# A two-layer hybrid decoder on one core: first products of a weight unit copied between PSUM banks, gates summed in PSUM, and another order of products

## The chip, the core and the metric

The kernel runs on one core of a Trainium2 chip, as one program for the whole computation. The metric is the device time of one execution in microseconds (us). The core has in-order engines that work side by side: TensorE (PE) multiplies matrices and adds the products up in PSUM banks, VectorE (DVE) does sums and differences, ScalarE (ACT) does copies, casts and the silu, GpSimd (POOL) and SyncE (SP) do the rest, SP mostly issuing DMAs of weights. An engine that has come to an instruction whose input isn't ready waits there, with all that is queued behind it.

## What is computed

Two decoder layers on 16 meta tokens and 512 tokens (528 in all, of width 1024), float32. The change touches the FFN alone:

```python
def hybrid_layer(h, ...):
    ...
    h = h + jnp.einsum('blc,cd->bld', mix, w_out)
    hn = rmsnorm(h, ffn_norm_g)
    ff = jax.nn.silu(jnp.einsum('bld,df->blf', hn, w_gate)) * jnp.einsum('bld,df->blf', hn, w_up)
    return h + jnp.einsum('blf,fd->bld', ff, w_down)
```

The width of `ff` is 2816. Ahead of it in a layer stand an RMSNorm, an input projection, attention with forgetting gates beside retention in chunks, and the output projection `w_out`. After the second layer come a last RMSNorm and the drop of the meta tokens. Layer 0 computes 528 tokens and layer 1's FFN the 512 that are returned.

## The kernel before

**Precision.** Each float32 matrix is split into a hi part (a cast on ScalarE: `whi`, `fwhi`, `th`, `ah`) and a lo part (the rest, a difference on VectorE: `wlo`, `fwlo`, `tl`, `al`), and each product is three matmuls: hi by hi, hi by lo, lo by hi. The weights' tiles lie in two rings, `whi`/`wlo` with two slots and `fwhi`/`fwlo` with three, between which the list of jobs alternates. When TensorE's program comes to a job's first matmul, `need` converts the jobs that come next in the list (L941 the cast, L942 the difference).

**Units.** The 2816 columns are 22 tiles f of 128, each with a gate and an up part. Tiles 0 and 1 are computed plainly (L231, finished at L895 and L896). Tiles 2 to 21 are *units*: gate and up together by seven products in place of eight, in a scheme of Strassen's kind over two halves of the width and two halves of the tokens (264 tokens each in layer 0, 256 in layer 1). A product (`product`, L953) is 12 matmuls, four steps of the width by three. Its weights are one of four forms: w1 the gate weights (`make1`), w2 (`make2`, L1084 and L1085), w3 (`make3`, L1092) and w4 (`make4`, L1098). Its right sides are halves of the normed input or forms of it (`x_forms`, L905 to L919, eight times ahead of the units: a scaled copy on ScalarE, four sums on VectorE, a split).

A unit has three PSUM banks: x, from the pool `psa` of four single banks, and z and y, the two of one tile of the pool `psd` of two tiles. The first product goes to x and is kept in memory by ScalarE (`keep`, L1117); x goes on to collect further products and is kept twice more; z and y collect one and two products. At the end `done` (L1127) takes z and y plus the kept copies as the gate (`sg`, L1131 and L1133), silu, multiplies it with the up part (L1136, L1138, L1139), and splits the result into `ah` and `al`.

**Fills.** The down projection of a group of tiles (`ROUNDS`) is spread between the products of the next group's units. In the groups f = 2 to 9 and 14 to 17 a unit carries two regular fills d0 and d1: `place` copies a slice of h into PSUM banks (p0 and p1, L1191 or L1193), the chunks of six matmuls add to it (L1207; two chunks for f = 2 to 5, four for the others), and ScalarE copies it back (L1214 or L1216). In the groups f = 10 to 13 and 18 to 21 the fill is a `Pair`, again seven products in place of eight, of six matmuls each (d0 to d6), whose results VectorE adds to h (L1036 to L1041). The down projection of the last group runs behind the units, in layer 0 with L1207 and in layer 1 as the tail, with `product` and the last norm woven in.

**Order.** TensorE's order is written out by hand in the loop at L1229 to L1265: x and z of the two first units ahead (x z x z), then for each unit (its own x and z first, from f = 4 on) x2 (w2), y (w2), p0, x3 (w3), d0, x (w3), p1, y (w4), d1. The orders of VectorE, ScalarE and SP are made by the framework's scheduler from the order of the calls, the estimated times and the marks `high_priority`.

Of the kernel before, what the change touches and what calls it, by code (L numbers as in the profile page):

```python
# [10 lines left out]
F32 = mybir.dt.float32  # L11
F32R = mybir.dt.float32r
AF = mybir.ActivationFunctionType
ALU = mybir.AluOpType
# [27 lines left out]
def hybrid_kernel(ctx, tc, x_t, w_in, w_fl, w_out, w_gate, w_up, w_down, vecs, b_fg, rope, decay, mask, ident, out_t):  # L42
# [818 lines left out]
    def ffn(l, st, real, last):  # L861
# [43 lines left out]
        def x_forms(k):  # L905
            def go():
                if k == 0:
                    st["t"] = [[fft(f"t{p}{i}", shape=(128, 2, 4, w)) for p in "hl"] for i in range(2)]
                s = fft("S", F32, (128, 6, w), 2)
                a, b = ((h[k][:, c0:c1], h[HB + k][:, c0:c1]) for c0, c1 in HC)  # L910
                g0, g1 = vcol(V_FFN + l * NK + k), vcol(V_FFN + l * NK + HB + k)
                with tc.issue_after(st["scaled"].ins) if real else ExitStack():
                    nc.scalar.activation(s[:, 0:2], two(h[k]), AF.Copy, scale=g0)
                nc.vector.tensor_sub(s[:, 2], s[:, 1], s[:, 0])
                for i in range(2):
                    nc.vector.scalar_tensor_tensor(s[:, 3 + i], b[1], g1, s[:, 1 + i], ALU.mult, ALU.subtract)
                nc.vector.scalar_tensor_tensor(s[:, 5], a[1], g1, s[:, 4], ALU.mult, ALU.subtract)
                th, tl = (t[:, k % 2] for t in st["t"][k // 2])
                split(th, tl, s[:, 2:6])  # L919
# [72 lines left out]
        class Pair:  # L992
# [40 lines left out]

            def add(self, i, col, n):
# [20 lines left out]
        class Unit:  # L1055
# [4 lines left out]

            def rest(self):
                self.w2 = add_job(load=self.load, make=self.make2, n=NK)
                self.w3 = add_job(load=self.load, make=self.make3, n=NK)
# [48 lines left out]
            def keep(self, i):  # L1112
                def go():
                    if i == 0:
                        self.t["e"] = fft("e", F32, (128, 3, w), 2)
                    with tc.high_priority():
                        nc.scalar.copy(self.t["e"][:, i], self.t["x"][:, 0:w])  # L1117
                        if i == 2:
                            e3 = self.t["e"][:, 2]
                            y = self.t["y"][:, 0:w]  # L1120
                            if self.f < PLAIN + 2:
                                y = tt("sq")[:, 0:w]
                                nc.scalar.copy(y, self.t["y"][:, 0:w])
                            nc.vector.tensor_add(e3, y, e3)
# [520 lines left out]
```

## Time and profile before

| what | us |
|---|---|
| runs | 1253.14, 1255.43, 1255.62 |
| median | 1255.43 |
| profiled execution | 1253.98 |
| its span | 1252.2 |
| TensorE busy in it | 1238.8 |
| VectorE busy | 1033.8 |
| ScalarE busy | 786.5 |

The span is that of the core's instructions; the execution's time has 1.8 us around it. A page of the profile has the busy time of each engine, then the granted clock of TensorE and the loads in 40 slices, the chain of work that ended last, and the costliest groups of instructions. A row such as `922.20 0.68 DVE L895 ... tq<-psd,R 128x512` says: from 922.20 us on, for 0.68 us, VectorE ran an instruction of line 895, that wrote the tile `tq` from a PSUM tile and `R`. A bracket behind it tells how long the engine sat idle before, and what released it. An instruction's duration includes its ends, which overlap the next one, so that starts stand closer than durations. An `x12` at the end of a row of TensorE joins 12 matmuls.

### The profile page before, as it was taken

The numbers are of one execution on the slowest core, as the hardware profiler recorded it, in microseconds if no ns is written. First come the engines' busy times: TensorE is split into PE (matmuls) and PEld (weight loads), VectorE is DVE, ScalarE is ACT, GpSimd is POOL, SyncE is SP. The second block draws the span as 40 slices with busy tenths as digits, with TensorE's granted clock in tenths as the row PEclk, the third lists the DMA queues.
The fourth block names the chain that finished last, engine by engine and source line by source line (L and its number), as shares of the span: only waits on it lengthen the run. The fifth ranks groups of instructions, "written<-read, shape, count | busy, mean of one in ns | idle before, by whom it ended". The sixth has DMA issues, their size and how long they took to land.

```text
span 1252.2 us, 24704 instructions
## 1 busy us (share of the span) xinstructions
PE 1238.8 (99%) x9609; PEld 1203.0 (96%) x9609; DVE 1033.8 (83%) x1969; ACT 786.5 (63%) x1525; POOL 293.6 (23%) x568
## 2 busy tenths in 40 slices
PE   9999999999999999999999999999999999999997
PEld 8999999999999999999999988998899999999997
DVE  7887756889987999799876877567999789988996
ACT  7766655677765645565566665557767665556545
POOL 4555655440000000000045556554300000000000
PEclk9999999999999999999999999999999999999999
DMA  6222222122433233322312222221414333332322
GB/s 237 68 71 75 77 69 85 60 85 70 143 110 102 85 102 119 102 85 85 118 61 85 75 79 69 77 84 52 142 57 140 102 102 102 102 110 93 102 68 68
DMA packets 43349, 116.27 MB, mean 93 GB/s; under 512 B 5088, under 2 KB 9952, under 8 KB 43232
## 3 DMA queue, kind: packets, MB, share of 16 engines
q1 hardware_dynamic: 42800, 114.41, 28.8%
q8 instruction: 75, 1.23, 0.4%
q14 instruction: 42, 0.34, 0.1%
q10 hardware_dynamic: 432, 0.29, 0.1%
HBM read 112.58 MB, written 2.10 MB: 92 GB/s over the span
## 4 chain that ended last, share of the span: by engine, by line
PE 92%; DVE 4%; ACT 2%; DMA 1%; issue 0%; SPq 0%; ACTq 0%; DVEq 0%
PE psd L231 28%; PE psa L953 23%; PE psd L953 16%; PE psd L1207 8%; PE psa L231 5%; PE psa L1207 3%; PE psa L452 2%; PE psa L619 2%; PE psa L549 1%; PE psa L753 1%; PE psa L789 1%; DMA raw<-w_down 1%; DMA h<-x_t 1%; PE psa L312 0%; DMA raw<-w_in 0%
## 5 line engine op out<-in xcount | busy, mean ns | idle before, releaser
L208 POOL TENSOR_TENSOR wlo<-raw,whi 128x128 fp32r<-128x128 f32 x488 | 253.7, 554 | 214.2 <-ACT whi L204 196.5
L231 PE MATMUL psd<-xh,whi 128*128 128x264 f32 (+1 forms) x696 | 169.5, 313 | 0.0
L231 PE MATMUL psd<-xl,whi 128*128 128x264 f32 (+1 forms) x696 | 160.6, 300 | 0.4 <-DVE xl L351 0.4
L231 PE MATMUL psd<-xh,wlo 128*128 128x264 f32 (+1 forms) x696 | 160.8, 300 | 0.0
L231 PEld LDWEIGHTS psd<-xh,whi 128*128 128x128 f32 x696 | 112.3, 189 | 3.3 <-ACT whi L204 0.3
L231 PEld LDWEIGHTS psd<-xh,wlo 128*128 128x128 f32 x696 | 110.9, 188 | 4.4
L231 PEld LDWEIGHTS psd<-xl,whi 128*128 128x128 f32 x696 | 111.5, 189 | 3.4 <-DVE xl L351 0.8
L204 ACT CAST whi<-raw 128x512 fp32r<-128x512 f32 (+1 forms) x140 | 82.2, 612 | 33.1 <-PE psd L231 17.4
L941 ACT CAST fwhi<-raw 128x512 fp32r<-128x512 f32 (+2 forms) x88 | 66.0, 757 | 51.7 <-PE psd L953 30.1
L942 DVE TENSOR_TENSOR fwlo<-raw,fwhi 128x512 fp32r<-128x512 f32 (+2 forms) x88 | 75.1, 854 | 20.9 <-ACT fwhi L941 20.6
L127 POOL MEMSET kc<- 64x528 f32 x4 | 2.1, 534 | 367.5 <-PE psd L1207 367.4
L941 ACT CAST whi<-raw 128x1024 fp32r<-128x1024 f32 (+1 forms) x72 | 56.1, 788 | 26.2 <-PE psd L953 17.6
L1117 ACT COPY e<-psa 128x264 f32<-128x264 f32 (+1 forms) x120 | 44.9, 374 | 42.6 <-PE psa L953 42.6
L953 PE MATMUL psa<-th,fwhi 128*128 128x264 f32 (+1 forms) x248 | 70.6, 285 | 0.0
L953 PE MATMUL psa<-th,fwlo 128*128 128x264 f32 (+1 forms) x248 | 70.2, 283 | 0.0
L953 PE MATMUL psa<-tl,fwhi 128*128 128x264 f32 (+1 forms) x248 | 70.2, 283 | 0.0
L953 PE MATMUL psa<-th,whi 128*128 128x264 f32 (+1 forms) x232 | 65.5, 282 | 0.0
L953 PE MATMUL psa<-th,wlo 128*128 128x264 f32 (+1 forms) x232 | 65.4, 282 | 0.0
L953 PE MATMUL psa<-tl,whi 128*128 128x264 f32 (+1 forms) x232 | 65.4, 282 | 0.0
L566 ACT ACTIVATE pr<-pr,nmax 128x144 f32<-128x144 f32 (+1 forms) x64 | 36.8, 576 | 45.4 <-DVE nmax L553 26.0
L942 DVE TENSOR_TENSOR wlo<-raw,whi 128x1024 fp32r<-128x1024 f32 (+1 forms) x72 | 64.0, 891 | 1.1 <-ACT whi L941 0.9
L953 PE MATMUL psd<-xh,fwlo 128*128 128x264 f32 (+1 forms) x168 | 47.6, 283 | 0.0
(445 smaller groups left out, 4417.7 us busy)
## 6 DMA issues: line engine op xcount, KB each, us to landing
raw<-w_in SPq DMA_DIRECT2D x54, 512.0 KB, 3.5
raw<-w_gate SPq DMA_DIRECT2D x44, 512.0 KB, 3.6
fraw<-w_up SPq DMA_DIRECT2D x40, 512.0 KB, 3.5
raw<-w_down SPq DMA_DIRECT2D x80, 256.0 KB, 3.6
raw<-w_out SPq DMA_DIRECT2D x16, 512.0 KB, 3.5
h<-x_t SPq DMA_DIRECT2D x8, 264.0 KB, 5.1
dec<-decay SPq DMA_DIRECT2D x8, 264.0 KB, 2.8
raw<-w_up SPq DMA_DIRECT2D x4, 512.0 KB, 3.9
```

Source lines behind the costliest of these rows:

```text
L204: pin(nc.scalar.copy(hi, job["raw"][:, c0:c1]), pinned)
L208: pin(sub(lo[:, c:c + step], job["raw"][:, c0 + c:c0 + c + step], hi[:, c:c + step].bitcast(F32)), pinned)
L231: nc.tensor.matmul(ps[1][b][:, 0:c1 - c0], w[:, wk, :], x[:, c0:c1], start=(k == 0 and i == 0), stop=(k == n - 1 and i == 2))
L452: nc.tensor.transpose(ps[:, 128 * j:128 * j + 128], src[:, o:o + 128], idt)
L549: nc.tensor.matmul(sc[0:nq, 0:c1 - c0], qq[:, q0:q0 + nq], kk[:, c0:c1], start=(i == 0), stop=(i == 1))
L566: nc.scalar.activation(pr, pr, AF.Exp, bias=nmax[0:nq], scale=-1.0, accum_out=rsum)
L619: nc.tensor.matmul(po[:, c0:SEQ], v[:, j, :], pp[:, j, META + c0:T], start=(j == 0 and i == 0), stop=(j == 4))
L941: nc.scalar.copy(hi, src)
L942: nc.vector.tensor_sub(lo, src, hi.bitcast(F32))
L953: nc.tensor.matmul(bank()[:, 0:b.shape[-1]], a[:, o + k, :], b, start=(fresh and k == 0 and i == 0), stop=(k == n - 1 and i == 2), skip_gr ...
L1117: nc.scalar.copy(self.t["e"][:, i], self.t["x"][:, 0:w])
L1207: nc.tensor.matmul(v[:, 0:c1 - c0], a[:, s * n + k, :], b[:, c0:c1], start=(k == 0 and i == 0 and not kept), stop=(k == n - 1 and i == 2), ...
```

## The change

- **Kept by a copy from bank to bank.** A unit's first product x is copied by ScalarE into the bank z, and the second product adds to it. The first product of y is copied to memory (`e`), and then VectorE writes x + e into the bank y, and later x + e into `e`, the second up part. So z and y collect the whole gate in PSUM, and `gated` reads it with the scaling in one instruction (L1143 of the changed kernel) as soon as its last product is in, ahead of the unit's last product. A `Pair`'s first product is likewise copied from x to z, where VectorE added it before.
- **Order of a unit.** xx, y, z, p0, x2, d0, p1, x3, d1, y2, x4 with regular fills, and xx, d0, y, x2, z, d2, d1, d3, x3, d4, y2, d5, x4, d6 with a `Pair` (before: x, z, d0, x2, y, d2, x3, d1, d3, x, d4, y, d5, d6). Here y is w2, z w1, x2 w2, x3 w3, y2 w4 and x4 w3. The first two units' heads are x, x, z, z. In the job list the fill stands behind w2 and before w3.
- **Temporaries.** The tile `S` of `x_forms` has four parts in place of six (the scaled copy goes to a tile `z`), and `e` one part in place of three. The last norm's temporaries, which shared these tiles, are allotted to fit (not shown).

The matmuls are the same in number and form.

```diff
@@ -906,17 +906,18 @@
 ...
-                s = fft("S", F32, (128, 6, w), 2)
+                s = fft("S", F32, (128, 4, w), 2)
+                sc = two(tt("z"))
-                    nc.scalar.activation(s[:, 0:2], two(h[k]), AF.Copy, scale=g0)
+                    nc.scalar.activation(sc, two(h[k]), AF.Copy, scale=g0)
 ...
@@ -1031,6 +1032,11 @@
                     return self.t[n]
                 return go
 
+            def keep(self):
+                z, x = (self.bank(n)()[:, 0:w] for n in "zx")
+                with tc.high_priority():
+                    nc.scalar.copy(z, x)
+
 ...
@@ -1044,9 +1050,9 @@
 ...
-                return (product(self.w1, 0, b(0, 0), x, True, False, 2, self.add(0, 0, "x")),
+                return (product(self.w1, 0, b(0, 0), x, True, False, 2, self.keep),
                         product(self.w1, 4, form(r, 2), x, False, False, 2, self.add(0, 1, "x")),
-                        product(self.w1, 2, b(1, 0), z, True, True, 2),
+                        product(self.w1, 2, b(1, 0), z, False, True, 2),
                         product(self.w1, 6, form(r, 1), y, True, False, 2, self.add(1, 1, "y")),
                         product(self.w2, 0, form(r, 3), x, False, False, 2, self.add(1, 1, "x")),
                         product(self.w2, 4, b(1, 1), y, False, True, 2, self.add(0, None, "zy")),
@@ -1111,32 +1123,34 @@
 
             def keep(self, i):
                 def go():
-                    if i == 0:
-                        self.t["e"] = fft("e", F32, (128, 3, w), 2)
+                    z, y, x = (self.bank(n)()[:, 0:w] for n in "zyx")
                     with tc.high_priority():
-                        nc.scalar.copy(self.t["e"][:, i], self.t["x"][:, 0:w])
-                        if i == 2:
-                            e3 = self.t["e"][:, 2]
-                            y = self.t["y"][:, 0:w]
-                            if self.f < PLAIN + 2:
-                                y = tt("sq")[:, 0:w]
-                                nc.scalar.copy(y, self.t["y"][:, 0:w])
-                            nc.vector.tensor_add(e3, y, e3)
+                        if i == 0:
+                            nc.scalar.copy(z, x)
+                        elif i == 1:
+                            self.t["e"] = fft("e", F32, (128, 272), 2)[:, 0:w]
+                            nc.scalar.copy(self.t["e"], y)
+                        elif i == 2:
+                            nc.vector.tensor_add(y, x, self.t["e"])
+                        else:
+                            nc.vector.tensor_add(self.t["e"], x, self.t["e"])
                 return go
 
+            def gated(self):
+                sg = self.t["sg"] = tt("sg")
+                c = slice(t0, T)
+                with tc.high_priority():
+                    nc.vector.scalar_tensor_tensor(two(sg), self.t["zy"][:, :, 0:w], RSC, two(st["R"]), ALU.mult, ALU.mult)
+                silu(sg[:, c], None if self.f < NF - 1 else ROOTS if last else LOGS)
+                u = self.t["u"] = tt("tq")
+                nc.vector.scalar_tensor_tensor(u[:, c], sg[:, c], RSC, st["R"][:, c], ALU.mult, ALU.mult)
+
             def done(self):
-                e = self.t["e"]
-                sg = tt("sg")
-                with tc.high_priority():
-                    nc.vector.tensor_add(two(sg), self.t["zy"][:, :, 0:w], e[:, 0:2])
+                u = self.t["u"]
                 c = slice(t0, T)
-                nc.vector.scalar_tensor_tensor(sg[:, c], sg[:, c], RSC, st["R"][:, c], ALU.mult, ALU.mult)
-                silu(sg[:, c], None if self.f < NF - 1 else ROOTS if last else LOGS)
-                u = tt("tq")
-                nc.vector.scalar_tensor_tensor(u[:, c], sg[:, c], RSC, st["R"][:, c], ALU.mult, ALU.mult)
                 u2 = two(u)
                 nc.vector.tensor_mul(u2[:, 0], self.t["x"][:, 0:w], u2[:, 0])
-                nc.vector.tensor_mul(u2[:, 1], e[:, 2], u2[:, 1])
+                nc.vector.tensor_mul(u2[:, 1], self.t["e"], u2[:, 1])
 ...
@@ -1149,20 +1163,17 @@
                 token_forms(self.f, u2)
 
             def head(self):
-                x, y, z = (self.bank(n) for n in "xyz")
-                return (product(self.w1, 0, x_block(0, 0), x, True, False, done=self.keep(0))
-                        + product(self.w1, HB, x_block(1, 0), z, True, True))
-
-            def middle(self):
+                x, z = (self.bank(n) for n in "xz")
+                return (product(self.w1, 0, x_block(0, 0), x, True, False, done=self.keep(0)),
+                        product(self.w1, HB, x_block(1, 0), z, False, True))
+
+            def rows(self):
                 x, y = (self.bank(n) for n in "xy")
-                return (product(self.w2, 0, t_form(2), x, False, False, done=self.keep(1))
-                        + product(self.w2, HB, t_form(0), y, True, False)
-                        + product(self.w3, 0, t_form(1), x, False, False, done=self.keep(2)))
-
-            def tail(self):
-                x, y = (self.bank(n) for n in "xy")
-                return (product(self.w3, HB, t_form(3), x, False, True)
-                        + product(self.w4, 0, x_block(1, 1), y, False, True, done=self.done))
+                return (product(self.w2, HB, t_form(0), y, True, False, done=self.keep(1)),
+                        product(self.w2, 0, t_form(2), x, False, False, done=self.keep(2)),
+                        product(self.w3, 0, t_form(1), x, False, False, done=self.keep(3)),
+                        product(self.w4, 0, x_block(1, 1), y, False, True, done=self.gated),
+                        product(self.w3, HB, t_form(3), x, False, True, done=self.done))
 
@@ -1237,11 +1247,12 @@
-                for i in (f, f + 1) if f == PLAIN else (f,):
-                    if i not in units:
-                        units[i] = Unit(i)
-                        steps += units[i].head()
-                u = units[f]
+                if f == PLAIN:
+                    units = {i: Unit(i) for i in (f, f + 1)}
+                    heads = [u.head() for u in units.values()]
+                    steps += heads[0][0] + heads[1][0] + heads[0][1] + heads[1][1]
+                u = units.get(f) or Unit(f)
+                xx, z = ([], []) if f < PLAIN + 2 else u.head()
                 p, g0, g1 = fills.pop(0)
                 seven = r - 1 in SEVENTHS and p in SEVEN
                 after = r - 1 in SEVENTHS and p + 1 in SEVEN or r in SEVENTHS and f == f1 - 1 and 0 in SEVEN
@@ -1251,17 +1262,18 @@
                     pair.rest()
                     u.last()
                     jobs[u.w3]["reach"] = 5 if after else 4
-                    d, m, t = pair.steps(), u.middle(), u.tail()
-                    steps += d[0] + m[:NK] + d[2] + m[NK:] + d[1] + d[3] + t[:HB] + d[4] + t[HB:] + d[5] + d[6]
+                    d, (y, x2, x3, y2, x4) = pair.steps(), u.rows()
+                    steps += xx + d[0] + y + x2 + z + d[2] + d[1] + d[3] + x3 + d[4] + y2 + d[5] + x4 + d[6]
-                u.rest()
+                u.second()
                 j = down_job(p, g0, g1)
                 jobs[j]["reach"] = 4 if after else 3
+                u.third()
                 u.last()
                 (p0, d0), (p1, d1) = (down(j, s, 2 * p + s, g0, g1, b, True)
                                       for s, b in enumerate((not real or f < PLAIN + 2, f == PLAIN)))
-                m, t = u.middle(), u.tail()
-                steps += m[:NK] + [p0] + m[NK:] + d0 + t[:HB] + [p1] + t[HB:] + d1
+                y, x2, x3, y2, x4 = u.rows()
+                steps += xx + y + z + [p0] + x2 + d0 + [p1] + x3 + d1 + y2 + x4
             fills = [(p, f0, f1) for p in range(NK // 2)]
```

**First place: the start of layer 1's FFN.** On ScalarE, before, from the cast of the input form of the last step but one to the hi part of the second weight form of f = 2 (`e` keeps x, `psa<-h0` is p0):

```order
L155 CAST th1_12030<-S_12105 128x1024
L1117 COPY e_12181<-psa_12168 128x256
L155 CAST th1_12030<-S_12132 128x1024
L1191 COPY psa_12261<-h0_73 128x256
L1191 COPY psa_12262<-h0_73 128x256
L941 CAST whi_12161<-S_12163 128x1024
```

and in the changed kernel (L1129 is the copy of x into z, of the first and the second unit):

```order
L1202 COPY psa_12232<-h0_73 128x256
L1129 COPY psd_12165<-psa_12152 128x256
L1202 COPY psa_12233<-h0_73 128x256
L1129 COPY psd_12187<-psa_12174 128x256
L155 CAST th1_12010<-S_12115 128x1024
L155 CAST ah1_12133<-tq_12130 128x512
L942 CAST whi_12145<-S_12147 128x1024
```

The two copies, of which the second waits for the second unit's x, now both stand ahead of the casts `th1`, `ah1` and `whi`. On VectorE, before, from the product of the plain tile 1 (L895) to the lo part of that weight form:

```order
L895 SCALAR_TENSOR_TENSOR tq_12146<-psd_12113,R_12018 128x512
L1084 TENSOR_TENSOR S_12163<-fraw_12070 128x512
L917 SCALAR_TENSOR_TENSOR S_12132<-h7_80,vec_84,S_12132 128x256
L1085 TENSOR_TENSOR S_12163<-S_12163,raw_12068 128x512
L1092 TENSOR_TENSOR fraw_12070<-raw_12068,fraw_12070 128x512
L155 TENSOR_TENSOR tl1_12031<-S_12132,th1_12030 128x1024
L896 TENSOR_TENSOR tq_12146<-tq_12146,sg_12102 128x512
L942 TENSOR_TENSOR wlo_12162<-S_12163,whi_12161 128x1024
```

and in the changed kernel:

```order
L895 SCALAR_TENSOR_TENSOR tq_12130<-psd_12096,R_11998 128x512
L917 SCALAR_TENSOR_TENSOR S_12115<-h7_80,vec_84,S_12115 128x256
L155 TENSOR_TENSOR tl1_12011<-S_12087,th1_12010 128x1024
L918 SCALAR_TENSOR_TENSOR S_12115<-h7_80,vec_84,S_12115 128x256
L1096 TENSOR_TENSOR S_12147<-fraw_12051 128x512
L896 TENSOR_TENSOR tq_12130<-tq_12130,sg_12084 128x512
L1097 TENSOR_TENSOR S_12147<-S_12147,raw_12049 128x512
L155 TENSOR_TENSOR tl1_12011<-S_12115,th1_12010 128x1024
L1104 TENSOR_TENSOR fraw_12051<-raw_12049,fraw_12051 128x512
L943 TENSOR_TENSOR wlo_12146<-S_12147,whi_12145 128x1024
```

The lo part `wlo` has two scaled steps (L917, L918) and a split of 1024 columns (`tl1_12011`) more behind L895 than before, and make3's step (L1104) still ahead of it.

**Second place: VectorE around the unit f = 4 of layer 1.** Before, from the lo part of w3 of f = 4, behind the gate of f = 3, to the sum x + y of f = 4 (L1124); `raw_12589` and `fraw_12591` are the weights of f = 5:

```order
L942 TENSOR_TENSOR wlo_12504<-fraw_12425,whi_12503 128x1024
L1085 TENSOR_TENSOR S_12626<-S_12626,raw_12589 128x512
L1136 SCALAR_TENSOR_TENSOR tq_12482<-sg_12478,R_12018 128x512
L942 TENSOR_TENSOR wlo_12571<-raw_12423,whi_12570 128x512
L1138 TENSOR_TENSOR tq_12482<-psa_12201,tq_12482 128x256
L1139 TENSOR_TENSOR tq_12482<-e_12214,tq_12482 128x256
L1092 TENSOR_TENSOR fraw_12591<-raw_12589,fraw_12591 128x512
L1098 TENSOR_TENSOR raw_12589<-raw_12589,S_12626 128x512
L155 TENSOR_TENSOR al3_12487<-tq_12482,ah3_12486 128x512
L942 TENSOR_TENSOR fwlo_12669<-fraw_12591,fwhi_12668 128x1024
L1124 TENSOR_TENSOR e_12521<-psd_12523,e_12521 128x256
```

and in the changed kernel, up to the sum that goes to the bank y of f = 4 (L1134). Directly ahead of these rows stand the lo part `fwlo_12504` of w3 of f = 4 (128x1024) and the gate of f = 3 (L1143, 128x512). `raw_12569` and `fraw_12571` are the weights of f = 5, `raw_12733` and `fraw_12735` those of f = 6:

```order
L943 TENSOR_TENSOR fwlo_12574<-raw_12569,fwhi_12573 128x1024
L1146 SCALAR_TENSOR_TENSOR tq_12461<-sg_12458,R_11998 128x512
L943 TENSOR_TENSOR wlo_12485<-raw_12481,whi_12484 128x512
L1152 TENSOR_TENSOR tq_12461<-psa_12174,tq_12461 128x256
L1153 TENSOR_TENSOR tq_12461<-e_12365,tq_12461 128x256
L1097 TENSOR_TENSOR S_12605<-S_12605,raw_12569 128x512
L1104 TENSOR_TENSOR fraw_12571<-raw_12569,fraw_12571 128x512
L155 TENSOR_TENSOR al3_12478<-tq_12461,ah3_12477 128x512
L1110 TENSOR_TENSOR raw_12569<-raw_12569,S_12605 128x512
L1096 TENSOR_TENSOR S_12769<-fraw_12735 128x512
L943 TENSOR_TENSOR wlo_12550<-raw_12405,whi_12549 128x512
L1097 TENSOR_TENSOR S_12769<-S_12769,raw_12733 128x512
```

The lo part of 1024 columns of w3 of f = 5 (`fwlo_12669`) stood ahead of the sum and no longer does; the first steps of f = 6 (L1096, L1097 on `S_12769`) stood behind it and now stand ahead. TensorE's next product into the bank x can only start when the sum is done.

**Third place: VectorE at the end of layer 1's units.** Before, up to the gate of the last unit (`sg_15954`; `raw_16007` is the down weight of the tail's second job):

```order
L942 TENSOR_TENSOR fwlo_15939<-raw_15935,fwhi_15938 128x1024
L1041 TENSOR_TENSOR h7_80<-psa_15828,h7_80 128x256
L942 TENSOR_TENSOR fwlo_16011<-raw_16007,fwhi_16010 128x1024
L1131 TENSOR_TENSOR sg_15954<-psd_15810,e_15808 128x512
L1039 TENSOR_TENSOR h6_79<-psd_15869,h6_79 128x512
```

and in the changed kernel (`sg_15903` the gate, `raw_15967` that weight):

```order
L943 TENSOR_TENSOR fwlo_15888<-raw_15884,fwhi_15887 128x1024
L1136 TENSOR_TENSOR e_15805<-psa_15756,e_15805 128x256
L1047 TENSOR_TENSOR h7_80<-psa_15776,h7_80 128x256
L1143 SCALAR_TENSOR_TENSOR sg_15903<-psd_15769,R_11998 128x512
L1045 TENSOR_TENSOR h6_79<-psd_15783,h6_79 128x512
L943 TENSOR_TENSOR fwlo_15971<-raw_15967,fwhi_15970 128x1024
```

The gate stood behind the lo part `fwlo` of the tail's second job, and now stands ahead of it, with a sum for h between.

More of the change, by code (lines that the diff above doesn't have):

```diff
@@ L1059, in __init__, with second, third @@
                 self.w1 = add_job(load=self.load, make=self.make1, n=NK)
+            def second(self):
+                self.w2 = add_job(load=self.load, make=self.make2, n=NK)
+            def third(self):
+                self.w3 = add_job(load=self.load, make=self.make3, n=NK)
             def rest(self):
-                self.w2 = add_job(load=self.load, make=self.make2, n=NK)
-                self.w3 = add_job(load=self.load, make=self.make3, n=NK)
+                self.second()
+                self.third()
             def last(self):
@@ L1230, in ffn @@
         fills = []
-        units = {}
         for r, (f0, f1) in enumerate(ROUNDS):
@@ L1389, in after_2 @@
                 sums(fin["va"], fin["a"][0:2])
-                fin["ra"], fin["ta"] = (fft("e", F32, (128, T), 2)[:, 0:na] for _ in range(2))
+                fin["ra"], fin["ta"] = (fft("e", F32, (128, 272), 2)[:, 0:na] for _ in range(2))
                 root(fin["ra"], fin["va"])
```

14 lines of the change are left out of this document (7 added, 7 removed).

## The prediction, made before the changed kernel had run

> **What bounds the kernel now.** I read the page first: the busy shares and the granted clock.
>
> ```profile
> span 1252.2 us, 24704 instructions
> ...
> PE 1238.8 (99%) x9609; PEld 1203.0 (96%) x9609; DVE 1033.8 (83%) x1969; ACT 786.5 (63%) x1525; POOL 293.6 (23%) x568
> ...
> PEclk9999999999999999999999999999999999999999
> ```
>
> TensorE is busy for 99% of the span at full clock, so the time is the number of matmuls times their pace, plus the few microseconds in which TensorE waits. The change keeps every matmul: it reorders products and moves sums between engines. So only two things can move the time: a wait of TensorE that goes, or one that comes. The view of TensorE's waits lists those of today:
>
> ```profile
> PE psd L953 <- DVE sg L1131: 1.8, 1, 1.8
> ...
> PE psd L1207 <- DVE al L155: 0.2, 1, 0.2
> ...
> PE psd L1207 <- ACT ah L155: 0.2, 1, 0.2
> ```
>
> (waiting line, what it waited for, total, times, longest). The other rows lie outside the FFNs, and the change does not touch them. So at most some 3 us can be won, and everything else it does can only be hidden or cost. VectorE is the cover that I doubt. Busy time by stretch (columns: us, busy PE, PEld, DVE, ACT, POOL, clock, DMA share, GB/s) shows it full where units are paired with seven-product fills, and full at the start of layer 1's FFN:
>
> ```profile
> 922.00:930.00 8.00, 8.00 (x67) 7.83 (x66) 8.00 (x12) 5.57 (x10) 0.00 (x0) 1.00 0.01 2
> ...
> 1045.00:1103.00 58.00, 58.00 (x495) 58.00 (x495) 57.91 (x104) 31.21 (x51) 0.00 (x0) 1.00 0.33 108
> ```
>
> So a step that comes later on VectorE, or is needed earlier by TensorE, shows as a wait unless it has slack.
>
> **Term 1, the wait in layer 1's tail goes: -1.9.** The chain of waits and TensorE's timeline there:
>
> ```profile
> 1211.68 4.54 DMA raw<-w_down
> ...
> 1217.40 1.22 DVE fwlo L942
> 1218.62 0.61 DVE sg L1131
> ...
> 1217.23 0.28 PE L953 MATMUL psa<-sqh,wlo 128*128 128x256 f32 x1
> 1219.28 0.39 PE L953 MATMUL psd<-ah,whi 128*128 128x272 f32 x1 [1.77 <-DVE sg L1131]
> ```
>
> The tail's first product needs the pair of banks that the last unit's gate holds. The sum that frees it (`sg`, L1131) is ready to run, but stands on VectorE behind the lo part of a down weight whose DMA lands at 1211.68 + 4.54 = 1216.2. TensorE's matmuls of this shape start 0.12 apart, so the loss is 1219.28 - 1217.23 - 0.12 = 1.93. After the change the gate is read from the banks directly, and in VectorE's order it stands ahead of that conversion (third place above). Its banks are also complete one product earlier. What is late next is the conversion itself: with its row's 1.22 it still ends at 1218.6, and its weights are those of the tail's second job, used 24 matmuls or 2.9 us after the first. With the first at 1217.35 that is 1220.2, so nothing waits. I take -1.9; if the conversion were needed at once, none of it would be won.
>
> **Term 2, the end of layer 0's FFN: -0.9.**
>
> ```profile
> 614.88 0.40 PE L1207 MATMUL psd<-ah,wlo 128*128 128x264 f32 x2
> 615.47 0.51 PE L1207 MATMUL psd<-ah,whi 128*128 128x264 f32 x2 [0.18 <-ACT ah L155]
> 616.21 0.51 PE L1207 MATMUL psd<-al,whi 128*128 128x264 f32 x2 [0.23 <-DVE al L155]
> 616.56 0.40 PE L1207 MATMUL psd<-ah,wlo 128*128 128x264 f32 x2
> ```
>
> Pairs otherwise start 0.24 apart, so 615.47 and 616.21 are late by 0.35 and 0.50, and 616.56 by 0.11: 0.96 in all, of which I take 0.9. The activations of the last tile are late because gate, silu, product and split run one after the other behind the unit's last product. After the change the gate is complete one 12-matmul product (1.45 us) earlier, so that its scaling, silu and `u` run under that product and the last fill, and only two VectorE products and the split stand behind the unit's end. Range: -0.9 to 0.
>
> **Term 3, the start of each FFN: +1.2 twice.** Now the two first units' heads run x, x, z, z, and then y of the second weight form comes at once, where x2 came. Both y and x2 need `wlo` of that form. Layer 1 before, chain and VectorE's timeline:
>
> ```profile
> 926.38 1.43 PE psd L953 x12
> 927.81 1.65 PE psa L953 x12
> ...
> 922.20 0.68 DVE L895 SCALAR_TENSOR_TENSOR tq<-psd,R 128x512 f32<-128x512 f32 x1
> 922.80 0.68 DVE L1084 TENSOR_TENSOR S<-fraw 128x512 f32<-128x512 f32 x1
> 923.40 0.48 DVE L917 SCALAR_TENSOR_TENSOR S<-h,vec,S 128x256 f32<-128x256 f32 x1
> 923.79 0.68 DVE L1085 TENSOR_TENSOR S<-S,raw 128x512 f32<-128x512 f32 x1
> ...
> 925.00 1.22 DVE L155 TENSOR_TENSOR tl<-S,th 128x1024 fp32r<-128x1024 f32 x1
> ...
> 926.74 1.22 DVE L942 TENSOR_TENSOR wlo<-S,whi 128x1024 fp32r<-128x1024 f32 x1
> 927.88 1.22 DVE L942 TENSOR_TENSOR fwlo<-fraw,fwhi 128x1024 fp32r<-128x1024 f32 x1
> ...
> 923.58 0.37 ACT L1117 COPY e<-psa 128x256 f32<-128x256 f32 x1 [3.61 <-PE psa L953]
> ```
>
> `wlo` ends at 927.96, and the third matmul of the product at 927.81 wants it at 928.05 (two steps of 0.12): just in time, and that product took 1.65 where the one before took 1.43, so 0.2 is waited already. By starts, one VectorE step of 1024 columns takes 1.14 (926.74 to 927.88), one of 512 takes 0.60 (922.20 to 922.80), one scaled step of 256 takes 0.39. In the order of the changed kernel VectorE does, from `u` of the dense tile (L895, which TensorE releases at the same 922.8) on: scaled step 0.4, `tl` 1.15, scaled step 0.4, first form step 0.6, L896 0.6, second form step 0.6, the second `tl` 1.14, make3's step 0.6, `wlo` 1.15. That is 922.8 + 6.6 = 929.4, 1.5 later than before. So y waits 1.4 where x2 waited 0.2: +1.2. ScalarE gives no better: its copy of the second head's x waits for that product (two products after 922.1, at 925.0) and stands before the casts `th`, `ah`, `whi` in its order. Layer 0 has the same rows:
>
> ```profile
> 310.99 1.46 PE psd L953 x12
> 312.45 1.47 PE psa L953 x12
> ...
> 306.82 0.70 DVE L895 SCALAR_TENSOR_TENSOR tq<-psd,R 128x528 f32<-128x528 f32 x1
> ...
> 309.21 1.22 DVE L942 TENSOR_TENSOR wlo<-S,whi 128x1024 fp32r<-128x1024 f32 x1
> ```
>
> There `wlo` ended at 310.4 and was wanted at 312.69, a slack of 2.3. After the change the form steps, the second `tl` and make3's step stand ahead of it as in layer 1: 307.4 + 6.5 = 313.9, so again +1.2. Bounds for each: 0, if the scheduler's order leaves VectorE idle nowhere and the casts come early; 2.4, if the copy on ScalarE holds the casts for one more product.
>
> **Term 4, y = x + e in the early regular units: +1.6.** The sum of the x and y banks (after's L1134) is now written into the y bank before x3 may overwrite x: x3 waits for it, and between x2 and x3 there is only one fill, d0. Before, x was copied on ScalarE and the sum had until the unit's end. For the sum itself I take the nearest row, and for 256 columns at unit stride 0.34 by starts:
>
> ```profile
> 997.03 0.42 DVE L1124 TENSOR_TENSOR e<-psd,e 128x256 f32<-128x256 f32 x1
> 997.37 0.68 DVE L1098 TENSOR_TENSOR raw<-raw,S 128x512 f32<-128x512 f32 x1
> ```
>
> For f=4 of layer 1 VectorE has, from the end of y2 of f=3 to the sum, in the second place above: the rest of a `fwlo` (0 to 1.14, I take 0.9, as it is called for by an earlier product), the gate 0.6, a `fwlo` 1.14, nine more steps of 512 columns at 0.60, two of 256 at 0.34, and the sum 0.42: 9.1. TensorE has x4, xx, y, z, x2 and d0 (two chunks of six), six times 1.42 to 1.43 (the row at 926.38): 8.5. So x3 waits 0.6. f=5 has the same steps: +0.6. In layer 0 a product takes 1.46 (the row at 310.99), 8.8, and most of VectorE's steps are as long, so f=4 waits +0.4 and f=5, whose rest is shorter, nothing. From f=6 on the fills have four chunks a product, 1.4 us more room, so none. Bounds: 0 to 2.4 (rest of 0, or of 1.14 in all four).
>
> What hides the rest: in units with seven-product fills VectorE loses the 512-column sum L1131 (0.6) and a pair's sum, and gains two of 256, so it gets about 0.3 shorter there. ScalarE takes two copies a unit for three. Copies from bank to bank do not occur in this trace; the nearest, bank to memory, is the row of 0.37 at 923.58, and memory to bank is this:
>
> ```profile
> L1191 ACT COPY psa<-h 128x264 f32<-128x264 f32 x26 | 9.8, 385 | 0.0
> ```
>
> I take 0.38 for it. A bound from below is 0.3, from above the 0.77 of both in turn. z, which now adds to the copied x, comes a product of 1.42 after xx, and so has 1.0 to spare.
>
> [...]
>
> **Sum.** -1.9 - 0.9 + 1.2 + 1.2 + 1.6 = +1.2 against the profiled execution's 1253.98 (span 1252.2 and 1.8 around it): 1255.2. That execution is among the fast ones: the runs are 1253.14, 1255.43 and 1255.62, and the mean of the four is 1254.5. I add the sum there: **1255.7**.
>
> **Rivals.**
> - *The new waits do not come* (faster). The scheduler may fit `wlo` in, and the rest of `fwlo` may be zero. For it: each of the three is under 1.5 us. Against: VectorE has no idle time in 922 to 930. Then -1.9 - 0.9 = -2.8: 1251.7.
> - *ScalarE is late between d0 and d1 in layer 1* (slower). There the two fills of a regular unit share one pair of banks. Before:
>
> ```profile
> 999.15 1.44 PE psa L953 x12
> ...
> 999.24 0.59 ACT L1216 COPY h<-psd 128x512 f32<-128x512 f32 x1 [2.51 <-PE psd L1207]
> 999.86 0.59 ACT L1193 COPY psd<-h 128x512 f32<-128x512 f32 x1
> 1000.50 1.05 ACT L941 CAST fwhi<-raw 128x1024 fp32r<-128x1024 f32 x1
> ```
>
>   Copy out and placing end 1.30 after d0 (999.15 to 1000.45). Two products lay between, 2.9; now it is x3 alone, 1.44. It fits with 0.1 to spare if ScalarE is free at d0's end. It decides at 0.1 of other work there; behind a whole cast of 1.05, as the one at 1000.50, d1 waits 0.95 in each of ten units (f = 4 to 9 and 14 to 17): 9.5, with the sum 1265.2. For it: the margin. Against: ScalarE sat idle 2.51 before this copy.
> - *The sum y = x + e is late in the four-chunk units too* (slower): the same mechanism at 0.4 in 16 units, 6.4 more: 1262.
> - *The tail's wait stays* (the change does not do what it says): VectorE's gate is ready but a step ahead of it waits. Then 1.9 is not won: 1257.6.
>
> **How the numbers follow.** Chances: forecast with its terms between half and double 0.58, no new waits 0.16, ScalarE late 0.12 (partly: 1258 to 1265), the sum late everywhere 0.06, the tail's wait stays 0.08. Term bounds alone give 1254.5 - 2.8 = 1251.7 to 1254.5 - 1.9 + 4.8 + 2.4 = 1259.8. The range 1251.7 to 1260 leaves out most of the two large rivals and a little below. About 0.2% (2.5 us) is what a measurement of this kernel can tell from no change. Faster by that needs nearly all of the first rival: 0.15. Slower by that takes the three slow rivals and the upper part of the forecast: 0.31. Same: 0.54.
>
> **What would show it.** Right: no wait on `sg` in the tail, none on `ah` and `al` at layer 0's end; new rows of TensorE waiting for VectorE's `wlo` by about 1.2 at 313 and 928, and at x3 for the sum in f = 4 and 5. Wrong: waits at d1 for ScalarE's placing in layer 1, waits at x3 in many units, or a start of the FFN without a gap. TensorE's matmuls starting further apart than 0.12 in stages without waits would break the argument altogether.

## The result, and the profile after

| kernel | median us | against before, 95% interval |
|---|---|---|
| before, in the same job | 1254.84 | |
| changed | 1303.36 (1303.25 to 1303.86) | 1.0389 (1.0371 to 1.0407) |

The change makes the kernel 3.9% slower. The prediction said 1255.7, from 1251.7 to 1260. Three of its four terms came out about as worked out, and a loss of some 48 us that it did not have came on top. The head of the page of the changed kernel answers to that of before:

```profile
span 1301.5 us, 24740 instructions
...
PE 1255.3 (96%) x9609; PEld 1207.3 (93%) x9609; DVE 1024.8 (79%) x1953; ACT 776.6 (60%) x1497; POOL 295.2 (23%) x568
```

The matmuls are as many as before, and VectorE and ScalarE do less. The span is 49.3 us longer, and the share of TensorE fell from 99% to 96%: time went into waits. The view of TensorE's waits names them (waiting line, releaser: us in total, times, longest):

```profile
PE psd L954 <- ACT psd L1129: 11.5, 20, 0.9
PE psd L954 <- DVE psd L1134: 10.9, 16, 1.2
PE psd L954 <- ACT e L1132: 10.7, 20, 0.8
PE psd L954 <- DVE wlo L943: 1.9, 2, 1.2
```

The first three are new and stand in no term of the prediction; the fourth is its term 3. There are 20 regular units from f = 4 on and 16 units with a `Pair`, over both layers, so every one of them waits. TensorE's timeline of the unit f = 6 of layer 1, with the last matmul of xx, the first of y, the last of y and the first of z:

```profile
1003.87 0.28 PE L954 MATMUL psa<-xh,wlo 128*128 128x256 f32 x1
1004.65 0.39 PE L954 MATMUL psd<-th,fwhi 128*128 128x256 f32 x1 [0.50 <-ACT psd L1129]
...
1006.06 0.28 PE L954 MATMUL psd<-th,fwlo 128*128 128x256 f32 x1
...
1006.85 0.39 PE L954 MATMUL psd<-xh,whi 128*128 128x256 f32 x1 [0.52 <-ACT e L1132]
```

and ScalarE's beside it:

```profile
1004.24 0.36 ACT L1129 COPY psd<-psa 128x256 f32<-128x256 f32 x1
...
1006.43 0.37 ACT L1132 COPY e<-psd 128x256 f32<-128x256 f32 x1 [1.32 <-PE psd L954]
```

y writes the bank y and needs nothing of the copy that goes to the bank z, yet it starts 0.05 after that copy's end. z writes the bank z and needs nothing of the copy that reads the bank y, yet it starts 0.05 after that one's end. Start to start the two steps take 0.78 and 0.79 where 0.12 is normal. The next matmul comes 0.22 or 0.23 later in place of 0.12, so that each wait costs about 0.1 more than its gap, and the unit loses 1.55. In the units with a `Pair`, of which this is f = 12 of layer 1, z follows x2 at once, and behind x2 the sum y = x + e goes to the bank y. TensorE's timeline with the end of x2 and the start of z:

```profile
1108.87 0.28 PE L954 MATMUL psa<-th,fwlo 128*128 128x256 f32 x1
1110.31 0.38 PE L954 MATMUL psd<-xh,whi 128*128 128x256 f32 x1 [1.16 <-DVE psd L1134]
```

and VectorE's:

```profile
1109.83 0.42 DVE L1134 TENSOR_TENSOR psd<-psa,e 128x256 f32<-128x256 f32 x1
```

Again the next product into one bank of the pair waits for an access to the other. Taken from the gaps, z's wait costs on average 0.90 a unit in layer 0 and 0.99 in layer 1. All 56 waits together cost 24.3 us in layer 0 and 23.6 in layer 1, 47.9 of the 49.3 that the span grew by. The four terms of the prediction came to about nothing together, and a smaller wait, in layer 1 at d1, makes up 1.9 (below).

### The profile page after: what moved, and what is told of

Its sections match the earlier page's. It is cut to its first block, busy times and chain, and to the rows that moved or that the text cites. A ratio compares the mean times of both kernels' runs of the same rounds, so it can differ in the third digit from the quotient of the medians.

```text
span 1301.5 us, 24740 instructions
## 1 busy us (share of the span) xinstructions
PE 1255.3 (96%) x9609; PEld 1207.3 (93%) x9609; DVE 1024.8 (79%) x1953; ACT 776.6 (60%) x1497; POOL 295.2 (23%) x568
## 4 chain that ended last, share of the span: by engine, by line
PE 77%; DVE 14%; ACT 6%; issue 2%; DMA 1%; DVEq 0%; ACTq 0%; SPq 0%
PE psd L231 27%; PE psa L954 14%; PE psd L954 13%; PE psd L1218 8%; PE psa L231 5%; PE psa L1218 2%; DVE fwlo L943 2%; DVE wlo L943 2%; PE psa L452 2%; PE psa L619 2%; PE psa L549 1%; PE psa L753 1%; DVE sg L1143 1%; ACT fwhi L942 1%; PE psa L789 1%
## 5 line engine op out<-in xcount | busy, mean ns | idle before, releaser
L231 PE MATMUL psd<-xh,whi 128*128 128x264 f32 (+1 forms) x696 | 169.7, 313 | 0.0
L954 PE MATMUL psa<-th,whi 128*128 128x264 f32 (+1 forms) x264 | 74.8, 283 | 0.0
L942 ACT CAST whi<-raw 128x1024 fp32r<-128x1024 f32 (+1 forms) x68 | 53.4, 796 | 35.7 <-PE psd L954 20.5
L954 PE MATMUL psa<-tl,whi 128*128 128x264 f32 (+1 forms) x264 | 74.5, 282 | 0.0
L954 PE MATMUL psa<-th,wlo 128*128 128x264 f32 (+1 forms) x264 | 74.4, 282 | 0.0
L943 DVE TENSOR_TENSOR wlo<-raw,whi 128x1024 fp32r<-128x1024 f32 (+1 forms) x68 | 61.0, 907 | 11.0 <-ACT whi L942 11.0
L954 PE MATMUL psa<-th,fwhi 128*128 128x264 f32 (+1 forms) x216 | 61.2, 283 | 0.0
L954 PE MATMUL psa<-tl,fwhi 128*128 128x264 f32 (+1 forms) x216 | 61.1, 283 | 0.0
L954 PE MATMUL psa<-th,fwlo 128*128 128x264 f32 (+1 forms) x216 | 61.1, 283 | 0.0
L954 PE MATMUL psd<-xh,fwhi 128*128 128x264 f32 (+1 forms) x168 | 49.4, 294 | 10.5 <-ACT e L1132 5.5
L954 PE MATMUL psd<-xh,whi 128*128 128x264 f32 (+1 forms) x152 | 44.8, 295 | 11.1 <-DVE psd L1134 5.8
```

The costliest lines, as they stand in the source:

```text
L231: nc.tensor.matmul(ps[1][b][:, 0:c1 - c0], w[:, wk, :], x[:, c0:c1], start=(k == 0 and i == 0), stop=(k == n - 1 and i == 2))
L942: nc.scalar.copy(hi, src)
L943: nc.vector.tensor_sub(lo, src, hi.bitcast(F32))
L954: nc.tensor.matmul(bank()[:, 0:b.shape[-1]], a[:, o + k, :], b, start=(fresh and k == 0 and i == 0), stop=(k == n - 1 and i == 2), skip_gr ...
```

## The experiments

Each ratio is to the kernel before as timed in the same job. The differences of medians in the text are mostly between jobs, in which the kernel before had medians from 1252.95 to 1254.84, so up to 2 us of one can be the job's. The theory: z and y are the two banks of **one tile**, and the program that the framework builds makes TensorE's next product into that tile wait for the last access of another engine to any part of it. The built program agrees: in the regular units from f = 4 on the first matmul of y waits for the semaphore count that the copy of x into z sets, and the first of z for the count of the copy of y into `e`. Before the change one such access stood between a unit's first product into the tile and its gate, the sum of L1124 that reads y. A fill and a product of x stood behind it, so that no wait showed in its trace.

| run | median us | ratio to before, 95% interval |
|---|---|---|
| e1, sum called later in units with a `Pair` | 1290.38 | 1.0298 (1.0277 to 1.0318) |
| e2, y in its own bank in layer 1 | 1278.00 | 1.0199 (1.0179 to 1.0219) |
| e3, reordered | 1259.80 | 1.0058 (1.0041 to 1.0075) |
| e4, e3 with S of six parts | 1259.25 | 1.0040 (1.0026 to 1.0053) |
| e5, e4 covered at three places | 1258.03 | 1.0031 (1.0020 to 1.0043) |
| e6, changed kernel with S of six parts | 1302.56 | 1.0385 (1.0366 to 1.0404) |
| e7, e5 covered at two more places | 1254.31 | 1.0003 (0.9994 to 1.0012) |
| e8, before with the last unit's gate earlier | 1249.80 | 0.9964 (0.9950 to 0.9977) |

**e1: the sum behind z.**

```diff
-                        product(self.w1, HB, x_block(1, 0), z, False, True))
+                        product(self.w1, HB, x_block(1, 0), z, False, True, done=self.keep(2) if late else None))
...
-                        product(self.w2, 0, t_form(2), x, False, False, done=self.keep(2)),
+                        product(self.w2, 0, t_form(2), x, False, False, done=None if late else self.keep(2)),
```

Here `late` holds in units with a `Pair`.

> Only in units with a Pair: the sum y = x + e is called behind z in place of ahead of it; TensorE's order stays as in the changed kernel. Theory (TensorE's next product into the tile of z and y waits for any earlier access to that tile, also of its other bank, so z waits for the sum into y): the 16 waits of z for the sum go, 0.90 each in layer 0 and 1.0 in layer 1 by the gaps, 15 us: about 1288. Rival (VectorE is full there, and whatever needs the sum next waits for it): the wait moves to x3, and the time stays near 1303.

13.0 us went, of the 15 expected (12.8 of them between the first and the last matmul of the units and the tail, both layers together), and the waits of z for the sum are gone. TensorE's waits in e1:

```profile
PE psd L954 <- ACT psd L1129: 11.5, 20, 0.9
PE psd L954 <- ACT e L1132: 10.4, 20, 0.5
PE psa L954 <- DVE xl L155: 2.0, 4, 0.6
```

The other two kinds stayed, and about the 2.0 missing came back as a wait of d1 for a form of the activations, which the order of the change needs earlier. TensorE's order, the sum and its place ahead of x3 are those of the changed kernel, so the sum's own length was not what z waited for.

**e2: y in a bank of its own.**

```diff
+                        elif real and self.f >= PLAIN + 2:
+                            self.t[n] = psum()[:, 0] if n == "z" else psum_a()
...
+                        for i, n in enumerate("zy"):
+                            nc.vector.scalar_tensor_tensor(two(sg)[:, i], self.t[n][:, 0:w], RSC, two(st["R"])[:, i], ALU.mult, ALU.mult)
```

> In layer 1 from f = 4 on the bank y is a tile of its own from the pool of single banks, and the gate is read in two instructions; TensorE's order and all copies and sums stay as in the changed kernel. Theory (the waits come of z and y being one tile): layer 1's waits of y and z go, 10 units by 1.55 us and 8 by 1.0: about 1280, and layer 0's stay. Rival (TensorE needs the copies' results, or ScalarE and VectorE come too late): no change, 1303. Rival (a copy or sum in a bank slows TensorE's writes to another bank): no change in the waits' total either.

1278.0, 25.4 less than the changed kernel. From the first to the last matmul of its units and tail, layer 1 takes 320.5 us where the changed kernel takes 345.4 and the kernel before 320.4; layer 0, which the edit leaves alone, stays at 330.3. TensorE's waits in e2 (L1131, L1134 and L1136 are the lines of the copy to z, the copy to `e` and the sum):

```profile
PE psd L954 <- ACT psd L1131: 6.5, 10, 0.9
PE psd L954 <- ACT e L1134: 5.2, 10, 0.5
PE psd L954 <- DVE psd L1136: 5.1, 8, 0.7
...
PE psa L954 <- DVE psa L1136: 0.6, 1, 0.6
```

The first three have half their number left, those of layer 0. In the unit f = 5 of layer 1 the copy into z starts at 987.60:

```profile
987.60 0.36 ACT L1131 COPY psd<-psa 128x256 f32<-128x256 f32 x1 [0.74 <-PE psa L954]
```

and TensorE goes from xx to y without a stop, and works in the bank y all through the copy:

```profile
987.22 0.28 PE L954 MATMUL psa<-xh,fwlo 128*128 128x256 f32 x1
987.34 0.28 PE L954 MATMUL psa<-th,whi 128*128 128x256 f32 x1
987.46 0.28 PE L954 MATMUL psa<-tl,whi 128*128 128x256 f32 x1
987.58 0.28 PE L954 MATMUL psa<-th,wlo 128*128 128x256 f32 x1
987.69 0.28 PE L954 MATMUL psa<-th,whi 128*128 128x256 f32 x1
```

The matmuls stay 0.12 apart. So neither the data, nor the copy's length, nor a copy at work in another bank makes TensorE wait; it is that the two banks are one tile. The last row of the waits above is the one place where a sum that came late on VectorE held x3, at a cost of 0.8 with the slow start (0.22 to the next matmul in place of 0.12). The other banks change the tiles that p0 and p1 get as well: p1 is placed before d0 is copied out (991.62 and 993.26 in f = 5), so that the smaller wait at d1 goes too. The sum of the three is 23.6 + 1.9 - 0.8 = 24.7, near the 24.9 by which layer 1 got shorter.

**e3: one tile again, and another order.**

```diff
+                if xx:
+                    j = down_job(p, g0, g1)
+                    u.second()
...
-                steps += xx + y + z + [p0] + x2 + d0 + [p1] + x3 + d1 + y2 + x4
+                    steps += [p0] + xx + d0 + y + [p1] + x2 + z + d1 + x3 + y2 + x4
```

> z and y are one tile again in both layers; the order puts other work behind each copy or sum: p0, xx, d0, y, p1, x2, z, d1, x3, y2, x4 in units with regular fills from f = 4 on, with the sum y = x + e called behind z in all units, and the fill's job ahead of w2. Theory: nearly all of the waits on copies and sums go, 20 units by 1.57 and 16 by 0.95, 47 us: about 1256.5. What is left against the kernel before are the starts of both FFNs (+3) and the two ends (-3). Rival (the time lies in the bank copies themselves, or in VectorE's load): over 1280.

1259.8: 43.6 went, of the 47 expected (42.8 between the first and the last matmul of the units and the tail, both layers together), with both banks in one tile. Something else stands between each copy or sum and the next product into the tile, and it covers the wait. What is left of waits:

```profile
PE psa L954 <- DVE e L1136: 2.4, 2, 1.7
PE psd L954 <- DVE wlo L943: 1.9, 2, 1.2
...
PE psa L954 <- DVE h L1047: 1.2, 1, 1.2
PE psd L1218 <- DVE al L155: 0.7, 1, 0.7
PE psa L1218 <- DVE al L155: 0.6, 1, 0.6
```

are the starts (`wlo`) and places at which this order needs a sum, a bank or the last activations too early.

**e4 and e6: the tile S of six parts again,** in e3 and in the changed kernel.

```diff
-                s = fft("S", F32, (128, 4, w), 2)
-                sc = two(tt("z"))
+                s = fft("S", F32, (128, 6, w), 2)
...
-                    nc.scalar.activation(sc, two(h[k]), AF.Copy, scale=g0)
+                    nc.scalar.activation(s[:, 0:2], two(h[k]), AF.Copy, scale=g0)
```

> The reordered kernel with x_forms' scaled copy back in a tile S of six parts, as before the change. Theory (the starts of both FFNs wait because the scaled copy now stands in the ring of general temporaries, waits there for a slot, and so brings the input forms and the weight form behind them late): the gaps at the two starts, 1.5 and 1.6 us, go but for the 0.2 that was there before: 2.9 less than 1259.8, 1256.9. Rival (the order x, x, z, z, y of the heads makes the wait, as the prediction had it): 1259.8.

> The changed kernel with x_forms' tile S of six parts alone. Theory (the ring of the scaled copy): the starts give back 2.9 us: 1300.4. Rival (the heads' order): 1303.3, with the gaps at both starts as they were.

The waits for `wlo` at both starts are gone from both kernels, though the heads' order x, x, z, z, y stayed. VectorE's timeline at the start of layer 1 shows it; first the changed kernel, from L895 to `wlo`:

```profile
946.44 0.69 DVE L895 SCALAR_TENSOR_TENSOR tq<-psd,R 128x512 f32<-128x512 f32 x1 [0.19 <-PE psd L231]
...
948.97 0.68 DVE L1096 TENSOR_TENSOR S<-fraw 128x512 f32<-128x512 f32 x1
...
952.52 1.22 DVE L943 TENSOR_TENSOR wlo<-S,whi 128x1024 fp32r<-128x1024 f32 x1
```

and then e6:

```profile
947.59 0.69 DVE L895 SCALAR_TENSOR_TENSOR tq<-psd,R 128x512 f32<-128x512 f32 x1
948.19 0.68 DVE L1095 TENSOR_TENSOR S<-fraw 128x512 f32<-128x512 f32 x1
...
952.12 1.22 DVE L942 TENSOR_TENSOR wlo<-S,whi 128x1024 fp32r<-128x1024 f32 x1
```

From L895 to `wlo` it is 6.1 in the first and 4.5 in the second: the weight form's first sum stands directly behind L895, and no longer behind the input forms. So the smaller temporaries make the start wait, not the heads' order. Whether it is the scaled copy's place in the ring of general temporaries or the size of S was not separated. The medians gave back less than the 2.9 expected, 0.6 in e4 and 0.8 in e6. The traces show where it went. From the first to the last matmul of the units and the tail, e6 is 1.5 shorter than the changed kernel in layer 1, but only 0.4 in layer 0, where a wait for p0 came in place of the one for `wlo` (0.8 from start to start, in both runs); e4 is 1.0 and 0.5 shorter than e3. The rest lies in the times ahead of the FFNs, which differ by 1 us and more between profiles of kernels with nearly the same code there; why they do stays open.

**e5 and e7: covering what e3 left.** e5, on top of e4 (the third place is p0's tile in layer 0's f = 14):

```diff
+                    if f == f0:
+                        steps += [p0] + xx + d0[:-1] + y + x2 + d0[-1:] + [p1] + z + d1 + x3 + y2 + x4
+                    elif f == f1 - 1 and len(d1) > 2:
+                        steps += [p0] + xx + d0 + y + [p1] + x2 + z + d1[:2] + x3 + d1[2:] + y2 + x4
```

> The kernel before this one with three places of the order mended: in the first unit of a regular group the last chunk of d0, which needs the activations of the unit just ahead, comes behind x2; in layer 0's f = 14 p0 goes to the tile of two banks; in the last units of the groups f = 6 to 9 and 14 to 17 half of d1 stands ahead of x3 and half behind. Theory (what is left of the loss are single waits at these places: 1.4 and 1.5 for activations, 1.5 for a bank, 1.8 and 0.9 for the sum into e): 7 us less than the kernel before this one, about 1250, and faster than the kernel before the change by some 2 to 3 us. Rival (VectorE and ScalarE are full, and mended waits come back elsewhere): 1254 to 1257.

It gave 1.2 of the medians, not 7, and the intervals of e4 and e5 overlap. The waits for activations and for the bank went, but two others remained or came:

```profile
PE psa L953 <- DVE e L1135: 2.2, 2, 1.8
PE psa L953 <- DVE xl L155: 1.9, 4, 0.6
```

The first stands on VectorE behind the conversion of a down weight that came late, as `sg` did in the tail before the change; the second is the wait that e1 had shown. e7, on top of e5:

```diff
-                    steps += xx + d[0] + y + x2 + z + d[2] + d[1] + d[3] + x3 + d[4] + y2 + d[5] + x4 + d[6]
+                    steps += xx + d[0] + y + x2 + z + d[2] + (d[3] + d[1] if f == f0 else d[1] + d[3]) + x3 + d[4] + y2 + d[5] + x4 + d[6]
...
-                    steps += y + [p0] + x2 + d0 + [p1] + x3 + d1 + y2 + x4
+                    steps += (([p0] + y) if f == PLAIN else y + [p0]) + x2 + d0 + [p1] + x3 + d1 + y2 + x4
```

> The covered kernel with d3 ahead of d1 in the first unit of each group with Pairs, and p0 of f = 2 ahead of y. Theory: the four waits of d1 for a form of the activations (0.65 and 0.65 in layer 0, 0.86 and 0.86 in layer 1, by the gaps) shrink by 0.7 each, and the wait for p0 in layer 0 (1.1) goes: 3.5 us less than 1258.0, 1254.5, about the time before the change. Rival (VectorE is full there and d4 or x3 waits in turn): 1257 to 1258.

1254.31, as expected, and no different from the kernel before. The waits for the form are gone from its trace, that for p0 is not. What remains of the change's design, as far as it was covered, is thus a gain at the ends that single waits elsewhere use up: from its first to its last unit matmul layer 0 is 1.3 longer than before the change, and layer 1 is 1.1 longer, although the 1.9 of its tail are won.

**e8: the kernel before with the last gate earlier.** This is one part of the change alone, without any copy from bank to bank.

```diff
+                if self.f == NF - 1:
+                    return (product(self.w4, 0, x_block(1, 1), y, False, True, done=self.gated)
+                            + product(self.w3, HB, t_form(3), x, False, True, done=self.done))
```

Here `gated` is the first half of `done`, down to `u`.

> The kernel before the change, with one part of the change alone, in the last unit f = 21 of each layer: the product y (w4) comes ahead of the last product of x (w3), and gate, silu and u are called behind it. Nothing is copied from bank to bank. Theory (terms 1 and 2 of the prediction): the wait of 1.9 on the gate in layer 1's tail and the 0.9 at layer 0's end go: 2.8 less than the kernel before, about 0.9978 of it. Rival (the lo part for the tail's second job, or w4 converted earlier, makes another wait): no difference.

1249.80, 0.9964 of the kernel before (0.9950 to 0.9977): the fastest of all. All of TensorE's waits in its view lie outside the FFNs:

```profile
PE psa L1485 <- DVE wide L64: 1.6, 1, 1.6
PE psa L619 <- DVE ptl L155: 0.6, 1, 0.6
PE psa L452 <- DVE nmax L553: 0.2, 1, 0.2
```

VectorE's timeline in the tail shows the gate ahead of the conversion that it stood behind:

```profile
1212.54 0.68 DVE L1131 TENSOR_TENSOR sg<-psd,e 128x512 f32<-128x512 f32 x1
...
1214.28 1.23 DVE L942 TENSOR_TENSOR fwlo<-raw,fwhi 128x1024 fp32r<-128x1024 f32 x1
```

## Why the prediction was wrong

- **What bounds the kernel: right.** Between waits TensorE's matmuls keep their 0.12, and nearly all of the 49.3 us are waits of TensorE.
- **Term 1 (-1.9): right.** The wait on `sg` is gone from the changed kernel, and layer 1 of e8, with this edit alone, is 2.1 shorter from its first unit matmul to its last (318.25 for 320.37).
- **Term 2 (-0.9): right.** The two gaps of layer 0's end are gone. e8 gave 4.2 of the medians for both ends, interval 2.9 to 6.3 by its ratio, against 2.8 for both terms. By the traces 0.9 of it lie ahead of layer 0's FFN, in code that e8 does not change; layer 1 gave 2.1, and the gaps at layer 0's end had cost 0.95.
- **Term 3 (+1.2 twice): the size was nearly right.** The gaps at the starts cost 1.5 and 1.7 where 0.2 was lost in each before, so +1.3 and +1.5. Part of the difference is a reading: the row of the chain at 927.81, by which the prediction dated the need for `wlo`, stands 0.17 behind that product's first start in the timeline (927.64). The steps on VectorE that delay `wlo` were the ones counted. That they stand there because of the smaller temporaries, and not because of the heads, is what e4 and e6 showed.
- **Term 4 (+1.6): not borne out.** No wait of x3 for the sum is in the view of the changed kernel, whose units are longer and so leave more time for it. In e2, where layer 1's are not, x3 waited once, 0.6, in f = 5.
- **The step that failed** is the paragraph "What hides the rest". It put the copy from bank to bank at 0.38, and its measured 0.36 agrees. It then asked only of z, the product that adds to the copied bank, whether the copy was done in time, and said that z "has 1.0 to spare". It did not ask of y. y follows xx at once and writes the other bank of the same tile, and the built program makes it wait for the copy. In the same way z waits for the copy that reads y, and in units with a `Pair` for the sum into y. For those units the paragraph had only counted VectorE's instructions, "about 0.3 shorter". Most of the waits cost 0.8 to 1.0 with the slow start behind them; there are 40 of the one kind and 16 of the other, 47.9 us in all.
- **The rivals** each had one mechanism of lateness on ScalarE or VectorE; none was that a product waits for an access that it does not need. The largest, 1265, was ScalarE late between d0 and d1 in layer 1, and it came in a small form that the view of waits is too coarse to list. In the unit f = 6 d0 ends, and x3 starts, at 1012.65; ScalarE copies d0 out and places p1, and d1's first matmul starts 0.05 after the placing (two rows of ScalarE's timeline and one of TensorE's):

```profile
1012.90 0.59 ACT L1227 COPY h<-psd 128x512 f32<-128x512 f32 x1 [1.96 <-PE psd L1218]
1013.52 0.59 ACT L1204 COPY psd<-h 128x512 f32<-128x512 f32 x1
...
1014.16 0.50 PE L1218 MATMUL psd<-ah,whi 128*128 128x256 f32 x2
```

  From x3's first start to the end of the placing it is 1.46 here, although ScalarE was idle, and x3 takes 1.42. The prediction had 1.30 with 0.1 to spare, because it took the end of d0 from a row of the chain (999.15), which stands 0.17 behind the start of the same matmul in the timeline of before (998.98): by that start it was 1.47 already. So d1 and its second matmul start about 0.1 late each, in nearly all of the ten units: 1.9 us in all, a second and much smaller term that the sum had at nothing.

## What to carry to other kernels

When a change makes another engine read or write part of a PSUM tile between two products, list every product that follows into any part of that tile, and put it behind other work or give the banks tiles of their own: here 56 such waits cost 47.9 us, a tile for y alone took 24.9 off layer 1 (e2), and other work in between took 42.8 off both layers (e3). The profile of before could not show these waits, but the changed program as built did: which semaphore count each first matmul of a product waits for, and whose it is. Where a change bundles several edits, a gain may sit in one of them: here the earlier last gate alone gains 0.36% (0.23% to 0.50%, e8), while the whole design, which has that gate too, is no faster than the kernel before even when most of its waits are covered (e7).

## What the runs showed of the hardware

A copy from one PSUM bank to another on ScalarE took 0.36 us for 128x256 in the changed kernel, about what one out of PSUM took (0.37 before the change). While it wrote a bank, TensorE's matmuls into another bank kept their 0.12 from start to start (e2). The sum x + y on VectorE, L1124 before the change, took 418 ns where it read y from a PSUM bank (median of 36) and 424 ns where it read y's copy in memory (median of 4).
